# A last layer norm split 704 to 320 columns, with weight and bias in two joined pairs of PSUM banks

## The chip, the cores and the metric

The kernel runs on one core of a Trainium2 chip. The metric is the device time of one launch in microseconds; lower is better. A core has five engines that run their own instruction streams and wait for each other: TensorE (PE, matrix products; its weight loads are shown as PEld), VectorE (DVE), ScalarE (ACT), GpSimd (POOL) and SyncE (SP, which issues most transfers here). [...]

## The reference

One decoder layer on x of 2048 rows x 1024 columns: two mixers, then a mixture of 32 experts, each half closed by a layer norm. The change touches the experts and the second norm:

```python
def hierarchical_moe(h, ...):        # two of the 32 experts for each row
    ...
    def expert_block(args):          # 128 rows of one expert
        xb, e = args
        hid = jax.nn.silu(xb @ w_gate[e]) * (xb @ w_up[e])      # 1024 -> 256
        return hid @ w_down[e]                                  # 256 -> 1024
    ...
# in reference():
        ffn = hierarchical_moe(h, ...)
        x = layer_norm(DEEP_ALPHA * x + gate2 * ffn, ln2_g[l], ln2_b[l])

def layer_norm(x, g, b):             # per row of 1024
    mu = x.mean(-1); var = square(x - mu).mean(-1)
    return (x - mu) * rsqrt(var + LN_EPS) * g + b
```

## The kernel before

The mixers fill the first 1205 us or so. Then `moe()` runs the 32 experts, and `tail()` the last norm.

**Experts.** A block is up to 128 rows of one expert. Every expert e has a block 0; 15 of the 32 have rows enough for a second one, block 1. Whether they do is known only at run time, so all work of a second block stands in arms that are run or skipped (`when`, L1209; the branches are at L1211). A float32 product is done as three products of a high and a low half: a high half is a rounded copy made by ACT, a low half is the difference, made by DVE or POOL.

For a block, PE turns the 128 x 1024 rows into eight 128 x 128 transposes (`turn`, L1116) in two PSUM tiles pT0 and pT1 of four each. `turned` (L1120) then copies each half on ACT (xT_hi, L1125) and subtracts on DVE (xT_lo, L1126). `gate_up` (L1135) is 24 matmuls of 512 columns into pg0 for block 0 or pg1 for block 1. `hidden` is ACT's silu (L1142) and DVE's product (L1143, hid). `hidden_turn` (L1152) turns that into ph, `hidden_turned` splits it (L1158 on ACT, L1159 on DVE), `down` (L1168) is 12 matmuls into two of three tiles pd, and `put` (L1176) has DVE scale them into y in two halves, which POOL adds to memory (`scatter`, L1182). Beside that the weights of the next expert are split: four pieces gu_hi on ACT (L1092) and gu_lo on DVE (L1093), and two pieces dn on ACT (L1101) and POOL (L1102).

The order of the experts' work on each engine is that of the code (`manual_schedule`, L1668). For one expert e PE does gate_up of (e, 0), turn of (e+1, 0), the hidden_turn of (e-1, 1) if there is one, down of (e-1, 0), then, each if there is one, gate_up of (e, 1), down of (e-1, 1) and turn of (e+1, 1), then hidden_turn of (e, 0), and begins gate_up of (e+1, 0). DVE does hT_lo of (e-1, 0), three gu_lo, hid of (e, 0), the two xT_lo of (e+1, 0), the fourth gu_lo, the two y of (e-1, 0), then, each if there is one, hid of (e, 1), y of (e-1, 1) and xT_lo of (e+1, 1).

**Waits.** A tile framework derives the waits between engines from the tiles that instructions read and write. An instruction that depends on work of another engine waits until that engine's count has reached the place of that work. A skipped arm adds the same counts, in its engine's order.

**Last norm.** `tail()` has the 16 row tiles of 128 in SBUF in six groups (TAIL: 1, 2, 3, 4, 3, 3 tiles). For each group the mean and variance come from DVE or ACT, DVE works out the scale in short operations that end at L1525, in scratch columns in PSUM. Then each row tile of 1024 columns is shared: columns up to `TS` go to DVE in two operations (L1537: minus the mean and times g, then times the scale and plus b; g and b lie in pT0 and pT1, copied there by ACT at L1466), the rest are normalised by ACT (L1530) and multiplied by g and added to b by POOL in two operations (L1538). Then the tile is stored (L1540). Here only SP's order is fixed by hand; the other engines' order is set by the framework's scheduler.

Of the kernel before, what the change touches and what calls it, by code (L numbers as in the profile page):

```python
# [10 lines left out]
F32 = mybir.dt.float32  # L11
# [9 lines left out]
P = 128  # L21
D = 1024
SEQ = 2048
KD = D // P
# [11 lines left out]
NG = 4  # L36
NONE = 1 << 20
ADA = 0.4
TS, TAIL = 512, ((1, 1), (2, 1), (3, 1), (4, 1), (3, 1), (3, 1))
HS = 608  # L40

RA, RB, MH2, MH3, WO = 0.6, 1.0, 0.25, 0.5, 0.5
# [11 lines left out]
class Layer:  # L54
# [1135 lines left out]
    def moe(self):  # L1190
# [20 lines left out]
            with tc.If((masks[engines][e // 16] & (1 << e % 16)) > 0):  # L1211
                work()
        PE, AV, DVE, POOL = (E.PE,), (E.Activation, E.DVE), (E.DVE,), (E.Pool,)
        self.pgs = pgs = [self.pk.tile([P, 512], F32, name=f"pg{i}") for i in range(2)]
        self.phs = self.ph.tile([P, 2, P], F32, tag="ph", name="ph")
        self.pds = pds = [self.pk.tile([P, 512], F32, name=f"pd{i}") for i in range(3)]
        self.pTs = [self.pk.tile([P, 4, P], F32, name=f"pT{i}") for i in range(2)]
        self.gate2 = mc.tile([P, D], F32, name="gate2")
        second = [mc.tile([P, D], F32, name=f"hr1_{i}") for i in range(2)]
        hr = [self.hrp.tile([P, D], F32, tag="hr", name="hr") for _ in range(2)]  # L1220
# [3 lines left out]
        for j in range(2):  # L1224
            t = mc.tile([P, NE, 4], I32, name=f"idx{j}")
# [11 lines left out]
        rows, xT, hid, hT, y = {}, {}, {}, {}, {}  # L1237
# [218 lines left out]
    def tail(self):  # L1456

        nc = self.nc
        g, b = self.g2b2
# [1 line left out]
        junk, stats = (self.hrp.tile([P, D], F32, tag="hr", name=n) for n in ("junk", "stats"))  # L1461
        xs, groups = [], []

        rows = [t.rearrange("p a b -> p (a b)") for t in self.pTs]
        for t, r in zip(rows, (g, b)):
            act.activation(t, r[:, 0:TS], AF.Copy)  # L1466
        for i in range(NT // 4):
            x = self.t16([P, 4, D], name="tail_x")
            for j in range(4):
                t = 4 * i + j  # L1470
                nc.sync.dma_start(x[:, j], self.d_xa[t * P:(t + 1) * P])  # L1471
                xs.append(x[:, j])

        t, cols = 0, self.pgs[0]
        for n, nv in TAIL:
            f = stats[:, 64 * len(groups):64 * len(groups) + 64]
            c = cols[:, 16 * len(groups):16 * len(groups) + 16]
# [212 lines left out]
```

## Time and profile before

| | |
|---|---|
| median of 3 runs | 1768.59 us (1767.44 to 1770.77) |
| the profiled execution | 1770.56 us |
| its span | 1768.9 us, mean granted clock of PE 0.956 |
| busy, whole span | PE 1565.4 us (88%), DVE 1254.1 (71%), ACT 775.4 (44%), POOL 534.7 (30%) |
| experts, 1205 to 1672 us | PE 442.84 us of 467 |
| last norm, 1694 us to the end | PE 0 us |

The profile is that of one execution, with start and length of every instruction on each engine. A span runs from the first to the last of them; the execution's own time is a little longer. An idle time in brackets is the engine's wait just before a row, with what released it. PEclk is the clock that TensorE was granted, as a share of full speed.

### The profile page before, as it was taken

What the parts mean: (1) busy time and instruction counts of PE and PEld (TensorE: products, weight loads), DVE (VectorE), ACT (ScalarE), POOL (GpSimd) and SP (SyncE); (2) the same over time, 40 slices, a digit from 0 to 9 for tenths busy, and PEclk for the clock granted to TensorE, in tenths of its full rate; (3) what the DMA queues carried; (4) which work ended last, traced back from release to release, by engine and by line L of the source; (5) the groups of instructions that cost most, each with busy time, mean ns of one, the idle gap of its engine ahead of it and who ended that gap; (6) DMA issues with size and microseconds to landing.
All of it is one profiled execution on the core that took longest, in us unless ns stands there. A gap on an engine that the chain in (4) does not pass through costs nothing. (4 is left out here: it accounts for less than half of the span.)

```text
span 1768.9 us, 25248 instructions
## 1 busy us (share of the span) xinstructions
PE 1565.4 (88%) x7784; PEld 1261.1 (71%) x7784; DVE 1254.1 (71%) x3010; ACT 775.4 (44%) x1603; POOL 534.7 (30%) x441
## 2 busy tenths in 40 slices
PE   6899999998999999999889999957999989999800
PEld 4678877776777778888678888845777778778600
DVE  6777667766877987574688887665667686876554
ACT  4433455445233336344443322226545565554452
POOL 3200111021110003022320211215556675765517
PEclk9999999999999999999999999978999999999955
DMA  9553586455764758544477854347989998998464
GB/s 282 166 184 100 167 249 192 127 136 161 219 198 144 214 163 252 141 99 118 143 241 227 256 168 144 138 160 224 298 259 290 285 316 265 294 305 240 105 221 178
DMA packets 347943, 356.79 MB, mean 202 GB/s; under 512 B 49705, under 2 KB 283778, under 8 KB 347794
## 3 DMA queue, kind: packets, MB, share of 16 engines
q1 hardware_dynamic: 330546, 316.61, 56.4%
q0 software_dynamic: 17248, 38.37, 9.2%
q8 instruction: 71, 1.16, 0.3%
q14 instruction: 78, 0.64, 0.1%
HBM read 268.83 MB, written 101.79 MB: 210 GB/s over the span
## 5 line engine op out<-in xcount | busy, mean ns | idle before, releaser
L280 PE MATMUL acc<-hhi,w_hi 128*128 128x512 f32 x896 | 365.6, 409 | 7.4 <-ACT st L444 3.2
L280 PE MATMUL acc<-hlo,w_hi 128*128 128x512 f32 x896 | 360.6, 403 | 1.7 <-DVE hlo L337 1.0
L280 PE MATMUL acc<-hhi,w_lo 128*128 128x512 f32 x896 | 361.0, 403 | 0.0
L280 PEld LDWEIGHTS acc<-hhi,w_hi 128*128 128x128 f32 x896 | 171.3, 191 | 48.6 <-ACT st L444 4.1
L280 PEld LDWEIGHTS acc<-hlo,w_hi 128*128 128x128 f32 x896 | 170.7, 191 | 40.8 <-DVE hlo L337 2.4
L280 PEld LDWEIGHTS acc<-hhi,w_lo 128*128 128x128 f32 x896 | 170.9, 191 | 39.7 <-issue 1.7
L1093 DVE TENSOR_TENSOR gu_lo<-gu_raw,gu_hi 128x1024 fp32r<-128x1024 f32 (+1 forms) x132 | 179.7, 1404 | 24.1 <-ACT gu_hi L1092 15.7
L1102 POOL TENSOR_TENSOR dn<-dn_raw,dn 128x1024 fp32r<-128x1024 f32 x64 | 168.2, 2655 | 58.4 <-ACT dn L1101 56.1
L1135 PE MATMUL pg<-gu_hi,xT_hi 128*128 128x512 f32 x376 | 150.0, 399 | 1.2 <-ACT xT_hi L1125 1.2
L1135 PE MATMUL pg<-gu_hi,xT_lo 128*128 128x512 f32 x376 | 147.5, 392 | 0.1
L1135 PE MATMUL pg<-gu_lo,xT_hi 128*128 128x512 f32 x376 | 147.3, 392 | 0.0
L1092 ACT ACTIVATE gu_hi<-gu_raw 128x1024 fp32r<-128x1024 f32 (+1 forms) x132 | 129.0, 1035 | 4.6 <-PE mix L889 2.8
L1168 PE MATMUL pd<-dn,hT_hi 128*128 128x512 f32 x376 | 120.6, 402 | 6.2 <-PEq L1211 2.5
L453 DVE SCALAR_TENSOR_TENSOR cv<-st,cw,cv 128x512 f32<-128x512 f32 x144 | 108.5, 754 | 2.1
L1182 POOL DMA_INDIRECT d_xa<-y,idx x47 | 77.1, 1640 | 105.9 <-DVE y L1176 46.3
L889 PE MATMUL mix<-wo_hi,y_hi 128*128 128x512 f32 x256 | 105.1, 411 | 0.0
L889 PE MATMUL mix<-wo_hi,y_lo 128*128 128x512 f32 x256 | 103.6, 404 | 1.2 <-DVE y_lo L871 1.2
L889 PE MATMUL mix<-wo_lo,y_hi 128*128 128x512 f32 x256 | 103.5, 404 | 0.0
L347 ACT ACTIVATE w_hi<-raw 128x1024 fp32r<-128x1024 f32 x56 | 59.6, 1065 | 93.4 <-PE acc L280 75.5
L1126 DVE TENSOR_TENSOR xT_lo<-pT,xT_hi 128x512 fp32r<-128x512 f32 x94 | 60.6, 686 | 39.1 <-ACT xT_hi L1125 35.2
L575 POOL TENSOR_SCALAR_AFFINE_SELECT gam<-gam 128x512 f32<-128x512 f32 x16 | 11.2, 701 | 252.7 <-ACT gam L574 241.7
L1168 PEld LDWEIGHTS pd<-dn,hT_hi 128*128 128x128 f32 x376 | 67.1, 188 | 27.4 <-issue 7.0
(352 smaller groups left out, 3255.1 us busy)
## 6 DMA issues: line engine op xcount, KB each, us to landing
dn_raw<-in_w_down_dram SPq DMA_DIRECT2D x32, 1024.0 KB
gu_raw<-in_w_gate_dram SPq DMA_DIRECT2D x60, 512.0 KB
gu_raw<-in_w_up_dram SPq DMA_DIRECT2D x60, 512.0 KB
raw<-in_w_in_dram SPq DMA_DIRECT2D x56, 512.0 KB
ada_w<-in_w_ada_dram SPq DMA_DIRECT2D x96, 256.0 KB
qkvT<-cv SPq DMA_DIRECT2D x48, 256.0 KB
x_t<-in_x_dram SPq DMA_DIRECT2D x16, 512.0 KB
y_raw<-yT SPq DMA_DIRECT2D x16, 512.0 KB
```

The source lines that it names most:

```text
L280: self.nc.tensor.matmul(ps, a[:, k, :], b[q][:, k, :], start=k + n == 0, stop=k == KD - 1 and n == 2)
L347: nc.scalar.activation(hi, raw, AF.Copy)
L453: nc.vector.scalar_tensor_tensor(y, st[:, t:t + 512], self.cw4[:, j, t:t + 1], y, op0=OP.mult, op1=OP.add)
L575: nc.gpsimd.affine_select(gam, gam, pattern=[[0, H], [1, P]], compare_op=OP.is_ge, fill=0.0, base=0, channel_multiplier=-1)
L889: nc.tensor.matmul(ps, a[:, k, :], self.wo[n][b][:, k, :], start=i == 0, stop=i == 3 * KD - 1)
L1092: nc.scalar.activation(hi[:, c], r, AF.Copy)
L1093: i = nc.vector.tensor_tensor(lo[:, c], r, hi[:, c].bitcast(F32), op=OP.subtract)
L1102: nc.gpsimd.tensor_tensor(dn[:, 1, k], r[:, k], dn[:, 0, k].bitcast(F32), op=OP.subtract)
L1126: nc.vector.tensor_tensor(lo[:, c], pT[n], hi[:, c].bitcast(F32), op=OP.subtract)
L1135: self.nc.tensor.matmul(ps, a[:, k], b[:, k], start=n == 0, stop=n == 3 * KD - 1)
L1168: self.nc.tensor.matmul(ps[n], hT[a][:, k], dn[:, b, k, c], start=i == 0, stop=i == 5)
L1182: i = self.nc.gpsimd.indirect_dma_start(out=self.d_xa, out_offset=bass.IndirectOffsetOnAxis(ap=idx[:, 0:1], axis=0), in_=y, in_offset=None ...
```

## The change

`TS` goes from 512 to 704, so DVE takes 704 columns of a row in the last norm, ACT and POOL 320. [...] So the two tiles pT0 and pT1 become one tile `pT` of two banks, and pg0 and pg1 one tile `pg` of two banks, both used through half views by the experts as before. In the last norm g lies in the first 704 columns of pT and b in those of pg, and the scratch columns move from pg0 to pd0.

```diff
-TS, TAIL = 512, ((1, 1), (2, 1), (3, 1), (4, 1), (3, 1), (3, 1))
+TS, TAIL = 704, ((1, 1), (2, 1), (3, 1), (4, 1), (3, 1), (3, 1))
...
-        self.pgs = pgs = [self.pk.tile([P, 512], F32, name=f"pg{i}") for i in range(2)]
+
+        self.pg = self.pk.tile([P, D], F32, name="pg")
+        self.pgs = pgs = [self.pg[:, i * 512:i * 512 + 512] for i in range(2)]
         self.phs = self.ph.tile([P, 2, P], F32, tag="ph", name="ph")
         self.pds = pds = [self.pk.tile([P, 512], F32, name=f"pd{i}") for i in range(3)]
-        self.pTs = [self.pk.tile([P, 4, P], F32, name=f"pT{i}") for i in range(2)]
+        self.pT = self.pk.tile([P, KD, P], F32, name="pT")
+        self.pTs = [self.pT[:, 4 * i:4 * i + 4] for i in range(2)]
...
-        rows = [t.rearrange("p a b -> p (a b)") for t in self.pTs]
+        rows = [t[:, 0:TS] for t in (self.pT.rearrange("p a b -> p (a b)"), self.pg)]
         for t, r in zip(rows, (g, b)):
             act.activation(t, r[:, 0:TS], AF.Copy)
...
-        t, cols = 0, self.pgs[0]
+        t, cols = 0, self.pds[0]
```

No instruction is added or taken out, and lines behind the experts' tiles count three higher. What moves are waits. On PE, before, between the turn of a second block of the next expert (an arm that may be skipped) and the next expert's first gate_up matmul (the last two rows; hr_1 are the rows of the second block):

```order
L1116 MATMUL pT_11285<-ident,hr_1_11289 128x128 [waits DMASW6_49,DMASW3_49,DMASW7_49,DMASW2_49,DVE_49]
L1116 MATMUL pT_11285<-ident,hr_1_11289 128x128 x3
L1116 MATMUL pT_11286<-ident,hr_1_11289 128x128 [waits DVE_49]
L1116 MATMUL pT_11286<-ident,hr_1_11289 128x128 x3
L1211 UNCONDITIONAL_BRANCH
L1211 UNCONDITIONAL_BRANCH [waits PE_49]
L1152 MATMUL ph<-ident,hid 128x128 [waits DVE_49]
L1152 MATMUL ph<-ident,hid 128x128
L1135 MATMUL pg_11279<-gu_hi,xT_hi 128x512 [waits Activation_49]
L1135 MATMUL pg_11279<-gu_lo,xT_hi 128x512
```

The same place on PE now:

```order
L1116 MATMUL pT<-ident,hr_1_11287 128x128 [waits DMASW6_49,DMASW3_49,DMASW7_49,DMASW2_49,DVE_49]
L1116 MATMUL pT<-ident,hr_1_11287 128x128 x7
L1211 UNCONDITIONAL_BRANCH
L1211 UNCONDITIONAL_BRANCH [waits PE_49]
L1152 MATMUL ph<-ident,hid 128x128 [waits DVE_49]
L1152 MATMUL ph<-ident,hid 128x128
L1211 UNCONDITIONAL_BRANCH
L1135 MATMUL pg<-gu_hi,xT_hi 128x512 [waits DVE_49,Activation_49]
```

The gate_up into pg waited for ACT alone; now it waits for DVE too, up to the place where DVE reads pg for the hid of a second block, which stands behind y of the expert before.

On ACT, the split of a turned second block and what follows, before:

```order
L1211 COMPARE_AND_BRANCH
L1125 ACTIVATE xT_hi<-pT_11285 128x512 [waits DVE_49,PE_49,Activation_49]
L1125 ACTIVATE xT_hi<-pT_11286 128x512 [waits DVE_49,PE_49]
L1211 UNCONDITIONAL_BRANCH
L1211 UNCONDITIONAL_BRANCH [waits Activation_49]
```

The same place on ACT now:

```order
L1211 COMPARE_AND_BRANCH
L1125 ACTIVATE xT_hi<-pT 128x512 [waits DVE_49,PE_49,Activation_49]
L1125 ACTIVATE xT_hi<-pT 128x512 [waits DVE_49]
L1211 UNCONDITIONAL_BRANCH
L1211 UNCONDITIONAL_BRANCH [waits Activation_49]
```

The second copy waited for PE's transposes; now it waits for DVE, up to the xT_lo that reads the first half of the same tile. The same holds where the turned block is a block 0.

In the last norm the last rows of DVE before, around the scale of the last group (L1525):

```order
L1522 SCALAR_TENSOR_TENSOR stats<-pg_11279,stats 128x3 [waits DVE_49]
L1524 COPY pg_11279<-stats 128x3 [waits DVE_49]
L1537 SCALAR_TENSOR_TENSOR tail_x<-tail_x,stats,pT_11286 128x512
L1525 TENSOR_TENSOR stats<-pg_11279,stats 128x3 [waits DVE_49]
L1537 SCALAR_TENSOR_TENSOR tail_x<-tail_x,stats,pT_11286 128x512 x2
```

And now, three lines further down in the file:

```order
L1525 SCALAR_TENSOR_TENSOR stats<-pd_11281,stats 128x3 [waits DVE_49]
L1527 COPY pd_11281<-stats 128x3 [waits DVE_49]
L1540 SCALAR_TENSOR_TENSOR tail_x<-tail_x,stats,pg 128x704
L1528 TENSOR_TENSOR stats<-pd_11281,stats 128x3 [waits DVE_49]
L1540 SCALAR_TENSOR_TENSOR tail_x<-tail_x,stats,pg 128x704 x2
```

Two of DVE's 32 operations stand behind that scale in both.

## Rows read from the trace of the kernel before

**Rows 1.** Windows: stretch, us; busy of PE, PEld, DVE, ACT, POOL; clock; DMA.
```profile
1205.00:1672.00 467.00, 442.84 (x2115) 356.78 (x2116) 322.28 (x393) 256.08 (x369) 291.36 (x153) 1.00 0.88 270
1730.00:1745.00 15.00, 0.00 (x0) 0.00 (x0) 14.00 (x55) 7.32 (x11) 14.66 (x12) 0.50 0.37 147
```
**Rows 2.** Timeline from 1729.5 us: start, us, engine, line, operation, count.
```profile
1730.18 32.41 POOL L1538 TENSOR_TENSOR tail_x<-tail_x,ln 128x512 f32<-128x512 f32 x26 [3.35 <-ACT tail_x L1530]
...
1744.16 0.15 DVE L1525 TENSOR_TENSOR stats<-pg,stats 128x3 f32<-128x3 f32 x1
...
1744.35 2.23 ACT L1530 ACTIVATE tail_x<-tail_x,stats 128x512 f32<-128x512 f32 x3 [2.15 <-DVE stats L1525]
```
**Rows 3.** Lines of the last norm: operation, count; busy us, mean ns; idle before.
```profile
L1538 POOL TENSOR_TENSOR tail_x<-tail_x,ln 128x512 f32<-128x512 f32 x32 | 39.6, 1264 | 36.7 <-ACT tail_x L1530 36.0
L1537 DVE SCALAR_TENSOR_TENSOR tail_x<-tail_x,stats,pT 128x512 f32<-128x512 f32 x32 | 23.2, 735 | 0.2
L1530 ACT ACTIVATE tail_x<-tail_x,stats 128x512 f32<-128x512 f32 x16 | 11.9, 802 | 7.7 <-DVE stats L1525 7.7
```
**Rows 4.** Lines of the experts, 1205 to 1672 us.
```profile
L1102 POOL TENSOR_TENSOR dn<-dn_raw,dn 128x1024 fp32r<-128x1024 f32 x64 | 168.2, 2655 | 58.4 <-ACT dn L1101 56.1 <-DMA d_xa<-y,idx 2.0
L1126 DVE TENSOR_TENSOR xT_lo<-pT,xT_hi 128x512 fp32r<-128x512 f32 x94 | 60.6, 686 | 39.1 <-ACT xT_hi L1125 35.2 <-DVEq L1211 3.2 <-ACT gu_hi L1092 0.7
L1159 DVE TENSOR_TENSOR hT_lo<-ph,hT_hi 128x256 fp32r<-128x256 f32 x45 | 18.8, 419 | 8.5 <-ACT hT_hi L1158 4.3 <-DVEq L1211 3.3 <-ACT gu_hi L1092 0.9
```
**Rows 5.** Timeline of expert 14, 1411.4 to 1419.5 us.
```profile
1411.38 1.22 DVE L1093 TENSOR_TENSOR gu_lo<-gu_raw,gu_hi 128x1024 fp32r<-128x1024 f32 x1
1412.00 5.22 POOL L1102 TENSOR_TENSOR dn<-dn_raw,dn 128x1024 fp32r<-128x1024 f32 x2 [0.21 <-ACT dn L1101]
...
1414.39 1.08 ACT L1125 ACTIVATE xT_hi<-pT 128x512 fp32r<-128x512 f32 x2
...
1415.02 1.29 DVE L1126 TENSOR_TENSOR xT_lo<-pT,xT_hi 128x512 fp32r<-128x512 f32 x2 [0.95 <-ACT xT_hi L1125]
...
1415.59 1.06 ACT L1092 ACTIVATE gu_hi<-gu_raw 128x1024 fp32r<-128x1024 f32 x1
...
1416.69 1.61 DVE L1093 TENSOR_TENSOR gu_lo<-gu_raw,gu_hi 128x1024 fp32r<-128x1024 f32 x1 [0.38 <-ACTq L1211]
...
1418.23 1.27 DVE L1176 TENSOR_TENSOR y<-pd,gate 128x512 f32<-128x512 f32 x2
...
1418.49 0.48 PE L1135 MATMUL pg<-gu_hi,xT_hi 128*128 128x512 f32 x1
```
**Rows 6.** Timeline of expert 15, 1427.5 to 1433 us.
```profile
1427.77 3.24 DVE L1093 TENSOR_TENSOR gu_lo<-gu_raw,gu_hi 128x1024 fp32r<-128x1024 f32 x1 [0.38 <-ACTq L1211]
...
1429.66 0.48 PE L1135 MATMUL pg<-gu_hi,xT_hi 128*128 128x512 f32 x1
...
1430.93 1.27 DVE L1176 TENSOR_TENSOR y<-pd,gate 128x512 f32<-128x512 f32 x2
```
**Rows 7.** Timeline of expert 8, 1329.5 to 1337 us.
```profile
1335.16 1.27 DVE L1176 TENSOR_TENSOR y<-pd,gate 128x512 f32<-128x512 f32 x2
...
1336.37 0.48 PE L1135 MATMUL pg<-gu_hi,xT_hi 128*128 128x512 f32 x1
```
**Rows 8.** Timeline of expert 0, 1212 to 1216.5 us.
```profile
1214.52 1.29 DVE L1126 TENSOR_TENSOR xT_lo<-pT,xT_hi 128x512 fp32r<-128x512 f32 x2 [0.88 <-ACT xT_hi L1125]
...
1214.55 0.50 PE L1135 MATMUL pg<-gu_hi,xT_hi 128*128 128x512 f32 x1
```
**Rows 9.** Timeline of expert 13, 1399 to 1407.5 us.
```profile
1404.71 1.27 DVE L1176 TENSOR_TENSOR y<-pd,gate 128x512 f32<-128x512 f32 x2
...
1405.44 0.73 PE L1168 MATMUL pd<-dn,hT_hi 128*128 128x512 f32 x2
```
**Rows 10.** Timeline between experts 9 and 10, 1350.5 to 1353 us.
```profile
1352.03 0.48 DVE L1143 SCALAR_TENSOR_TENSOR hid<-pg,idx,hid 128x256 f32<-128x256 f32 x1 [2.98 <-ACT hid L1142]
...
1352.40 0.48 PE L1135 MATMUL pg<-gu_hi,xT_hi 128*128 128x512 f32 x1
```

## Prediction

> **What bounds the kernel now.** I read the windows view first, cut at the stages. In the 467 us of the experts the matmuls of PE are busy for 442.84 us, at a granted clock of 1.00, DVE for 322 and POOL for 291 [rows 1]: the experts are bound by PE, and every new wait of PE there is paid, unless PE would have waited anyway. In the last norm PE is idle. From 1730 to 1745 us POOL is busy for 14.66 of 15 us and DVE for 14.00 [rows 1]. The timeline then shows what ends last: POOL's 26 last additions and multiplications run without a gap for 32.41 us to 1762.59, while DVE has finished its last scale at 1744.31 [rows 2]. The span is 1768.9, so the last store and the end take 6.3 us after POOL. The last norm is bound by POOL, whose queue is still long when DVE is done.
>
> The profiled execution took 1770.56 us; the median is 1768.59, 1.97 lower. The sum below is a difference against the profiled execution and is then set on the median.
>
> **The last norm.** A half-row operation on POOL takes 1264 ns at 512 columns, on DVE 735, on ACT 802 [rows 3]. POOL goes from 512 to 320 columns. Its wider row, 1024 columns in 2655 ns [rows 4], shows no fixed share (2.59 ns a column against 2.47), so 320 columns are 0.79 us by proportion; I take 0.83. DVE gets 192 columns more. Two of its subtractions out of PSUM, 512 columns in 686 ns and 256 in 419 ns [rows 4], give 1.04 ns a column, so +0.20 us each, 0.94 in all. ACT's normalisation of 320 columns becomes some 0.63.
>
> 30 of DVE's 32 operations stand ahead of the last group's scale, as in the two order pieces of the tail: that scale moves from 1744.31 by 30 x 0.20 = 6.0 to 1750.3. ACT's first tile is ready at 1750.95. POOL has just caught up by then: it starts its run some 4 us later than 1730.18 (20 of the 30 operations lie ahead), and 20 operations of 0.83 end at 1750.8. Its last six, for three tiles, end at 1750.95 + 6 x 0.83 = 1755.9; with a hand-off at the start, 1756.1. Against 1762.59 that is **-6.5**. DVE becomes the last norm's bound.
>
> Bounds: if POOL's price did not shrink with the width, the tail would end as before plus POOL's later start, +4. If DVE's growth were hidden, the last scale stays at 1744.31 and POOL's six end at 1749.9, -12.7. No row shows DVE reading 704 columns across two banks. If the second bank costs a second start (419 ns less 256 x 1.04 is 0.15 us), the 30 operations give 4.5 back and -2 is left; nothing speaks for it, I take no cost. The two copies into PSUM are 192 columns longer and run before the rows arrive: nothing.
>
> **The joined tiles in the experts.** A tile is what the order of dependent work is kept by. Two half tiles were followed apart; a joined one is followed as one. The order pieces show two new waits.
>
> First, ACT's second half copy xT_hi now waits for DVE's xT_lo of the first half. At expert 14 the two copies took 1.08 us together from 1414.39, DVE's two 1.29 from 1415.02 [rows 5]. So the second copy can start only at 1415.02 + 0.69 [rows 4] = 1415.71 with a wake, and ends at 1416.35, 0.88 later than 1415.47. What stands behind it on ACT is the fourth gu_hi, and behind that on DVE the fourth gu_lo and then y.
>
> Second, PE's gate_up of the next expert waits for DVE up to the hid of a second block, which stands behind y of the previous expert; where there is no second block, the skipped arm releases it, and only once DVE has done y. Before, PE needed ACT's xT_hi alone and DVE could be late. Behind the waiting matmul stands all of PE's work.
>
> What a late y costs is read at expert 14: y ends at 1419.50, PE started the gate_up of 15 at 1418.49 [rows 5], so 1.01 of waiting, plus what the first wait adds. The fourth gu_lo would start at 1416.69 + 0.88 = 1417.57. It took 1.61 us, while one beside which POOL began late took 1.22, and it ended 1.08 after POOL's dn, which ran to 1417.22 [rows 5]. Started after that, it takes 1.22 and ends at 1418.79, 0.49 later than before; I use 0.47 everywhere.
> [...]
>
> With 0.1 for the release, the terms are:
> - Experts 14, 15 and 21, no turn of a second block between: 1.01 + 0.47 + 0.1 = 1.55 each, **4.65**. At 15 the plain reading is larger: y ended at 1432.20 and PE began at 1429.66 [rows 6], 2.54 late, behind a gu_lo of 3.24 us. But PE's waiting at 14 lets DVE catch up, so only the increase counts.
> - Experts 1, 8, 11, 16 and 22, where a turn of a second block takes PE's time: at 8, the one of the five that is shown, y ended at 1336.43 and PE began at 1336.37 [rows 7], 0.06 + 0.57 = 0.63. By the same pair of rows 11 gives 0.71 and 1 gives 0.91; 16 and 22, once what went before is paid, 0.6 each: **3.45**. At 30, y is early: nothing.
> - Expert 0, with no y: the xT_lo pair ends at 1215.81, PE began at 1214.55 [rows 8]; 1.26 + 0.88 + 0.1 = **2.2**.
> - Seven experts after one with a second block (4, 7, 10, 13, 20, 24, 29): the gate_up comes late enough, but the second half of the second block's down waits for the first half of y; at 13 y began at 1404.71 and the matmuls at 1405.44 [rows 9], right behind it. y is 0.47 later: **3.3**.
> - Three gate_ups right behind a hid of the second block, as at 1352.51 against 1352.40 [rows 10], 0.2 each: **0.6**.
>
> The sum is **+14.2**. Lower bound: the first wait is swallowed, and what is left is 1.01 three times, the small lateness of the others and 2.2 + 0.6, about 6.5. Upper bound: the lateness at 15 and at three more of that pattern, 16, 21 and 22 (2.54, 3.2, 2.65, 1.8 by the same pair of rows) stands in full with 0.88 each, 13.7, beside the 1.55 of 14, 2.2 for three others and the last three terms, 6.1: 23.6, about 24. PE has such short waits already with its clock at 1.00 over the stage [rows 1]; I charge no clock. Loads and POOL's gathers move along with PE.
>
> **Sum**: +14.2 - 6.5 = +7.7, 1778.3 for the profiled execution. On the median: **1776.3**.
>
> **Rivals.**
> 1. The lateness of DVE stands in full. For it: gu_lo of 3.24 us [rows 6] shows that POOL's dn can hold DVE, and after a shift it may hold it elsewhere. Against: PE's waits give DVE time. 1768.6 + 24 - 6.5 = 1786.
> 2. The waits are small, and the norm pays for them: the lower bound, 6.5 - 6.5, 1768.6, no change. For it: PE's shift moves the whole ring, and a place that is late once is early next.
> 3. The other side: the joined tiles bring no order. The two halves lie in different banks, and if the engines run beside each other in them, as xT_hi's second half and xT_lo's first do now from 1415.02 to 1415.47 [rows 5], only the norm counts: 1768.59 - 6.5 = 1762.1. It decides if PE's first matmul of an expert starts before y ends. Against it stand the waits in the order pieces.
> [...]
> 4. The norm's gain fails, by DVE's second start or POOL's price: 1768.6 + 14.2 - 2 to + 4, 1781 to 1787.
>
> **Chances.** The forecast 0.60; rival 1 0.14; rival 2 0.13; rival 3 0.08; rival 4 0.05. The forecast's own range is 1772 to 1782 (experts +10 to +20, norm -6.5). The range is 1765 to 1786: it goes down past rival 2 with a norm of -9 (1768.6 + 6.5 - 9 = 1766), and up to rival 1; rival 3 lies below, and little above. What can't be told from no change is 0.2%, 3.5 us. Slower: the forecast, rivals 1 and 4, 0.77 with a little lost to the forecast's lower edge, 0.76. Same: rival 2's, 0.13. Faster: 0.11, rival 3 and the low part of rival 2.
>
> **What would show it.** Right: PE waits ahead of the first gate_up matmul after experts 0, 1, 8, 11, 14, 15, 16, 21 and 22, released by DVE, 0.6 to 2.2 us each; ACT's two xT_hi apart by an xT_lo; the last down matmul some 14 us later; POOL's operation in the norm near 0.83 us, DVE's near 0.94, the norm 6.5 us shorter, with POOL done soon after DVE's last scale. Wrong: PE starts those matmuls while y runs; the experts' stage is as long as before; or POOL's operation stays above 1.1 us.

## The result

The changed kernel takes 1789.59 us (median of four, 1784.70 to 1795.56) against 1768.69 for the kernel before: a ratio of 1.0118, interval 1.0079 to 1.0158. It is slower, as forecast, but by about 21 us where 7.7 were forecast, and above the range of 1765 to 1786.

The profiled execution took 1795.56 us, 25.00 more than that of before. Cut at the first gate_up matmul of expert 0 and the last matmul of expert 31, the difference falls into three parts: expert 0's gate_up begins 6.42 us later (1211.70 against 1205.28), the experts take 502.42 us against 478.51 (1205.28 to 1683.79 in the kernel before; [rows 1] stops at 1672), +23.91, and what follows is 5.33 shorter. 6.42 + 23.91 - 5.33 = 25.00. The first part is not the change: the instructions of each engine ahead of the experts are the same in both, and in the runs below that start lies anywhere from 1198.5 to 1211.8, in kernels with and without the change. Why it moves these runs don't tell. It is a good part of the scatter between executions: a second profile of the changed kernel has that start 10.0 us earlier and took 1786.58 us, 9.0 less. So the experts are compared here by their own stretch.

The windows of the changed kernel, the whole of its experts first, then pieces around the wait at expert 14 (stretch, us; busy of PE, PEld, DVE, ACT, POOL; granted clock; DMA):

```profile
1211.70:1714.10 502.40, 462.81 (x2154) 369.23 (x2154) 319.35 (x401) 261.25 (x372) 290.94 (x155) 0.98 0.83 252
1432.90:1436.08 3.18, 0.55 (x4) 0.24 (x3) 2.49 (x4) 1.87 (x4) 0.21 (x1) 1.00 0.57 181
1436.08:1437.30 1.22, 1.22 (x5) 1.01 (x6) 0.50 (x2) 1.22 (x2) 1.15 (x1) 1.00 1.11 384
1437.30:1440.70 3.40, 3.40 (x9) 2.63 (x8) 3.33 (x3) 1.59 (x2) 2.79 (x3) 0.50 1.03 342
1440.70:1442.00 1.30, 1.30 (x7) 1.08 (x6) 0.00 (x0) 0.00 (x0) 1.28 (x2) 0.99 0.89 178
```

The clock over the experts was 1.00 in [rows 1]; it is 0.98 now. PE was busy for 0.55 of the 3.18 us up to the gate_up of expert 15. It began that at 1.00, and 1.2 us later, in the midst of dense work, fell to 0.50 for 3.40 us. The 24 matmuls of that gate_up took 7.31 us from first to last, against 5.72 before: 1.6 us lost behind the wait, about as much as the wait.

The timeline of expert 14 in the changed kernel, for [rows 5]:

```profile
1430.29 0.59 ACT L1125 ACTIVATE xT_hi<-pT 128x512 fp32r<-128x512 f32 x1
...
1430.91 0.69 DVE L1126 TENSOR_TENSOR xT_lo<-pT,xT_hi 128x512 fp32r<-128x512 f32 x1 [0.95 <-ACT xT_hi L1125]
...
1431.64 0.60 ACT L1125 ACTIVATE xT_hi<-pT 128x512 fp32r<-128x512 f32 x1 [0.76 <-DVE xT_lo L1126]
...
1432.27 0.69 DVE L1126 TENSOR_TENSOR xT_lo<-pT,xT_hi 128x512 fp32r<-128x512 f32 x1 [0.66 <-ACTq L1211]
1432.36 1.06 ACT L1092 ACTIVATE gu_hi<-gu_raw 128x1024 fp32r<-128x1024 f32 x1
1433.45 1.23 DVE L1093 TENSOR_TENSOR gu_lo<-gu_raw,gu_hi 128x1024 fp32r<-128x1024 f32 x1 [0.49 <-ACTq L1211]
...
1434.22 0.41 PE L1152 MATMUL ph<-ident,hid 128*128 128x128 f32 x2 [1.19 <-PEq L1211]
1434.59 1.28 DVE L1176 TENSOR_TENSOR y<-pd,gate 128x512 f32<-128x512 f32 x2
...
1436.08 0.47 PE L1135 MATMUL pg<-gu_hi,xT_hi 128*128 128x512 f32 x1 [1.44 <-ACT gu_hi L1092]
```

Both new waits are there: the two copies of xT_hi stand apart with an xT_lo between them, and PE begins 0.21 us after y has ended (1434.59 + 1.28 = 1435.87). Before, PE began 1.01 us ahead of that end. The releaser named in the last bracket, ACT's gu_hi, is only what came last in the profile; gate_up doesn't read that piece; what it follows is y, by 0.20 to 0.21 us at all eight gate_ups that come to wait for one. The gu_lo, which begins 0.34 us after POOL's dn has ended (1433.11), takes 1.23 us where it took 1.61.

For [rows 7], [rows 9] and [rows 8], the timelines of experts 8, 13 and 0:

```profile
1348.43 1.28 DVE L1176 TENSOR_TENSOR y<-pd,gate 128x512 f32<-128x512 f32 x2
1349.92 0.47 PE L1135 MATMUL pg<-gu_hi,xT_hi 128*128 128x512 f32 x1 [0.48 <-ACT xT_hi L1125]
...
1420.59 1.28 DVE L1176 TENSOR_TENSOR y<-pd,gate 128x512 f32<-128x512 f32 x2
1421.33 0.73 PE L1168 MATMUL pd<-dn,hT_hi 128*128 128x512 f32 x2 [0.43 <-DVE y L1176]
...
1222.42 0.69 DVE L1126 TENSOR_TENSOR xT_lo<-pT,xT_hi 128x512 fp32r<-128x512 f32 x1 [0.66 <-ACTq L1211]
...
1223.31 0.76 PE L1135 MATMUL pg<-gu_hi,xT_hi 128*128 128x512 f32 x1 [2.19 <-ACT hT_hi L1158]
...
1223.87 0.63 PE L1135 MATMUL pg<-gu_lo,xT_hi 128*128 128x512 f32 x1
```

At each PE begins just behind DVE. Matmuls of 0.63 us, as in the last row, are those at the clock of 0.50; at 1.00 they show 0.39, as in the same kernel's gate_up of 15 from 1440.95 on.

The last norm: its groups of instructions by line (busy us, mean ns), then the last scale and POOL's last 20 operations, for [rows 3] and [rows 2]:

```profile
L1541 POOL TENSOR_TENSOR tail_x<-tail_x,ln 128x320 f32<-128x320 f32 x32 | 27.1, 861 | 43.6 <-DVE pd L1506 28.3 <-ACT tail_x L1533 14.1
L1540 DVE SCALAR_TENSOR_TENSOR tail_x<-tail_x,stats,pT 128x704 f32<-128x704 f32 x16 | 14.9, 932 | 1.0 <-ACT junk L1496 0.7 <-issue 0.2
L1533 ACT ACTIVATE tail_x<-tail_x,stats 128x320 f32<-128x320 f32 x16 | 9.4, 644 | 15.0 <-DVE stats L1528 14.8
```

```profile
1769.97 17.62 POOL L1541 TENSOR_TENSOR tail_x<-tail_x,ln 128x320 f32<-128x320 f32 x20 [0.28 <-ACT tail_x L1533]
...
1780.67 0.16 DVE L1528 TENSOR_TENSOR stats<-pd,stats 128x3 f32<-128x3 f32 x1
```

DVE's wide operation takes 932 ns, as 735 and 192 columns of 1.04 ns make 935, so no price for the second bank is to be seen; POOL's 861, ACT's 644. The last scale ends 66.7 us after the experts' last matmul, POOL 73.5 us after it, against 78.8 before.

### The profile page after: what moved, and what is told of

The parts are those of the page before. It is cut to its first block, busy times and chain, and to the rows that moved or that the text cites. A ratio compares the mean times of both kernels' runs of the same rounds, so it can differ in the third digit from the quotient of the medians.

```text
span 1793.8 us, 25232 instructions
## 1 busy us (share of the span) xinstructions
PE 1581.3 (88%) x7784; PEld 1271.5 (71%) x7784; DVE 1252.0 (70%) x3010; ACT 777.2 (43%) x1603; POOL 516.6 (29%) x441
## 5 line engine op out<-in xcount | busy, mean ns | idle before, releaser
L1093 DVE TENSOR_TENSOR gu_lo<-gu_raw,gu_hi 128x1024 fp32r<-128x1024 f32 (+1 forms) x132 | 167.0, 1308 | 30.1 <-ACT gu_hi L1092 24.0
L1126 DVE TENSOR_TENSOR xT_lo<-pT,xT_hi 128x512 fp32r<-128x512 f32 x94 | 65.0, 692 | 75.6 <-ACT xT_hi L1125 58.9
L1135 PEld LDWEIGHTS pg<-gu_hi,xT_hi 128*128 128x128 f32 x376 | 73.0, 194 | 28.9 <-ACT gu_hi L1092 4.5
L1125 ACT ACTIVATE xT_hi<-pT 128x512 fp32r<-128x512 f32 x94 | 56.2, 598 | 80.4 <-DVE xT_lo L1126 39.8
```

The costliest lines, as they stand in the source:

```text
L1093: i = nc.vector.tensor_tensor(lo[:, c], r, hi[:, c].bitcast(F32), op=OP.subtract)
L1125: self.last_turn = nc.scalar.activation(hi[:, c], pT[n], AF.Copy)
L1126: nc.vector.tensor_tensor(lo[:, c], pT[n], hi[:, c].bitcast(F32), op=OP.subtract)
L1135: self.nc.tensor.matmul(ps, a[:, k], b[:, k], start=n == 0, stop=n == 3 * KD - 1)
```

## The experiments

The theory was that the experts lose some 24 us: 16 to 17 of waits of PE, and 7.2 because the clock falls behind the four longest of them. A rival was that the joined tiles slow the mixers, a second that the clock falls for another reason, a third that part of the loss is the norm's. Times of the experts below are from expert 0's first gate_up matmul to the last matmul, in the profile: 478.51 us before.

**The change again.**

> The changed kernel once more. Theory: the experts cost some 24 us more (about 16.5 us of new waits of PE on DVE and ACT, and 7.2 us because the granted clock falls to 0.50 for some 3 us behind the four longest waits), the last norm gives 5.3 back, and the 6.4 us by which the first transposes of the experts began later in the profiled run (1209.08 against 1202.66) are not the change but differ from run to run: median 1784 to 1796, and in this profile the first transpose stands anywhere from 1202 to 1210. Rival: the joined tiles also slow the mixers ahead of the experts; then the first transpose is at 1208 or later again.

Measured: 1789.13 us, ratio 1.0095 (1.0070 to 1.0121). Expert 0's gate_up began at 1201.70, 3.6 us earlier than in the kernel before (the first transpose, at 1199.08, even ahead of the stretch expected), and still the experts took 503.64 us, +25.1. The rival of slower mixers is out. The clock fell behind the same four gate_ups, which took 7.4 us more together, in other shares: 2.9 at 16 and 1.3 at 1.

**The joins alone.**

```diff
-TS, TAIL = 704, ((1, 1), ...
+TS, TAIL = 512, ((1, 1), ...
```

> Both joins, but TS stays 512, so the last norm is shared as before. Theory: the whole loss of the experts stands and the norm gives nothing back: the changed kernel plus 5.3, some 1768.7 + 24 = 1792 (1789 to 1799). Rival: part of the loss belongs to the wider rows of the norm; then it lies below the changed kernel.

Measured: 1795.88 us, ratio 1.0133 (1.0093 to 1.0172); experts 504.62 us, +26.1; POOL ended 80.0 us after the last matmul. The loss is there in full without the wide rows, so it is the joins', and the wide rows are worth 6.5 us (80.0 against 73.5).

**The wide rows without the joins.** The experts' PSUM pools are closed after `moe()`, and the norm opens one of its own:

```diff
+            with ExitStack() as ps:
+                self.ph = self.pool(ps, name="ph", bufs=1, space=PSUM)
+                self.pk = self.pool(ps, name="pk", bufs=1, space=PSUM)
...
+            self.pn = self.pool(st, name="pn", bufs=1, space=PSUM)
...
+        rows = [self.pn.tile([P, D], F32, name=n)[:, 0:TS] for n in ("g2", "b2")]
...
+        t, cols = 0, self.pn.tile([P, 512], F32, name="cols")
```

> TS is 704, but the experts keep their separate half tiles; the norm gets two PSUM tiles of two banks of its own once the experts' pools are closed. Theory: the experts are as before and the norm is 5.3 us shorter: 1768.7 - 5.3 = 1763.4 (1761 to 1766). Rival: the norm's gain needs the early copy of weight and bias into tiles that the experts free one by one, or the wide rows cost something else: 1768 or more.

Measured: 1767.49 us against 1773.19 for the kernel before, measured beside it, ratio 0.9974 (0.9953 to 0.9996). The experts took 479.11 us, as before, and POOL ended 72.1 us after them, 6.7 earlier. So the change's purpose can be had without its price.

**y ahead of the fourth gu_lo**, in the changed kernel:

```diff
-                for _ in su:
-                    pass
                 if e:
                     down(e - 1, 0)
                     out(e - 1, 0)
                     store(e - 1, 0)
+                for _ in su:
+                    pass
```

> The changed kernel, but y of the expert before stands ahead of the fourth gu_hi and gu_lo on ACT and DVE. Theory: PE's waits ahead of gate_up of experts 15, 16 and 22 (1.7, 1.6 and 2.8 us) fall below 0.7, the clock stays at 1.00 behind them (4.8 us), five waits of 0.7 and seven of 0.5 on y go too: some 15 us below the changed kernel, 1775 (1772 to 1780). Rival: the clock falls for a reason other than the length of PE's wait, or the fourth gu_lo is now late for the 18th matmul: 1782 or more.

Measured: 1778.32 us, ratio to before 1.0028 (1.0013 to 1.0043), 10.8 below the changed kernel measured beside it; one of its twelve executions took 7083.71 us, which I can't explain. So it came within the range expected, but not by the way expected. The seven downs behind y, 0.5 us longer in the changed kernel, are 0.1 to 0.2 shorter than in the kernel before. But PE still waited 1.42, 1.35 and 1.64 us ahead of gate_up of 15, 16 and 22, where less than 0.7 was expected, and still 2.24 ahead of that of 1, where there is no y. Its timeline at expert 14 shows why:

```profile
1423.02 1.29 DVE L1176 TENSOR_TENSOR y<-pd,gate 128x512 f32<-128x512 f32 x2 [0.23 <-PEq L1211]
...
1424.22 1.21 DVE L1093 TENSOR_TENSOR gu_lo<-gu_raw,gu_hi 128x1024 fp32r<-128x1024 f32 x1
...
1425.64 0.49 PE L1135 MATMUL pg<-gu_hi,xT_hi 128*128 128x512 f32 x1 [1.18 <-DVEq L1211]
```

PE now waits for the gu_lo, and begins 0.21 us behind its end: what it waits for is the skipped arm of the second block's hid, which stands behind whatever DVE does last. The windows around the two gate_ups of 15 and 22, from the end of the matmuls before:

```profile
1422.86:1425.64 2.78, 0.41 (x4) 0.23 (x3) 2.42 (x3) 1.47 (x3) 1.13 (x2) 1.00 0.79 245
1425.64:1426.00 0.36, 0.36 (x2) 0.32 (x3) 0.00 (x0) 0.36 (x2) 0.36 (x1) 0.93 1.09 373
1426.00:1429.30 3.30, 3.30 (x9) 2.57 (x8) 2.93 (x4) 2.72 (x3) 2.69 (x3) 0.50 1.08 384
```

```profile
1530.40:1533.40 3.00, 0.41 (x4) 0.24 (x3) 2.64 (x3) 1.69 (x3) 2.83 (x2) 1.00 0.86 256
1533.40:1539.00 5.60, 5.60 (x25) 4.57 (x26) 4.88 (x4) 2.98 (x4) 5.27 (x3) 1.00 1.01 341
```

Behind the first the clock fell to 0.50 within 0.4 us, and it fell at 1 and 16 too; behind the second, in which PE was idle for a little longer, it stayed at 1.00. How long PE waits does not settle by itself whether the clock falls.

**One join at a time**, on the kernel before.

```diff
-        self.pTs = [self.pk.tile([P, 4, P], F32, name=f"pT{i}") for i in range(2)]
+        self.pT = self.pk.tile([P, KD, P], F32, name="pT")
+        self.pTs = [self.pT[:, 4 * i:4 * i + 4] for i in range(2)]
```

> The kernel before with pT0 and pT1 joined and nothing else: ACT's second xT_hi half waits for DVE's first xT_lo half, PE's gate_up for ACT alone. Theory: only the seven places where the second half of a second block's down waits for y pay (0.5 each), and expert 1 at its start: 3 to 6 us in the experts, no wait over 1 us ahead of a gate_up after expert 1, and the clock stays. Rival: the serial halves on ACT and DVE are the main loss, 12 or more.

Measured: 1770.72 us, ratio 0.9997 (0.9977 to 1.0018). The experts took 485.28 us, +6.8 and a little above the forecast: 0.5 to 0.9 at the seven downs, 1.05 and 0.71 at two turns (behind the gate_ups of 17 and 22) that the forecast did not have, no wait of over 1 us ahead of a gate_up, no lower clock behind one. That it cost nothing in all is the norm: POOL ended 71.3 us after the experts, 7.5 earlier than before, at the same width. The scheduler, which orders all but SP there, had put ACT's first normalised tile further ahead, before sums of later groups; it began at 1708.58 where it was 1712.54, with the experts' last matmul at the same time in both:

```profile
1708.58 0.81 ACT L1531 ACTIVATE tail_x<-tail_x,stats 128x512 f32<-128x512 f32 x1
...
1722.60 32.52 POOL L1539 TENSOR_TENSOR tail_x<-tail_x,ln 128x512 f32<-128x512 f32 x26 [2.54 <-ACT tail_x L1531]
```

POOL's 26 last operations are as long as in [rows 2], but begin at 1722.60 where it was 1730.18.

```diff
-        self.pgs = pgs = [self.pk.tile([P, 512], F32, name=f"pg{i}") for i in range(2)]
+        self.pg = self.pk.tile([P, D], F32, name="pg")
+        self.pgs = pgs = [self.pg[:, i * 512:i * 512 + 512] for i in range(2)]
```

> The kernel before with pg0 and pg1 joined and nothing else: PE's gate_up waits for y, but y itself isn't made later. Theory: at experts 1, 15, 16 and 22 PE waits some 1.3, 1.1, 1.1 and 2.2 us, at the others 0.2 to 0.4, 7 to 9 in all, and the clock falls behind fewer than four of them: 8 to 14 us in the experts. Rival: the two waits bite only together, since PE waits where y is late by both; then it is below 4.

Measured: 1784.59 us, ratio 1.0073 (1.0046 to 1.0101); experts 492.55 us, +14.0, the upper end. PE waited 1.47, 1.22, 0.92 and 2.84 us at 1, 15, 16 and 22, and behind all four, not fewer, the gate_up took 1.2 to 2.5 us more, 6.9 together. So here waits of about 1 us cost as much again in clock. The two joins alone add up to 20.8 us; together they cost 23.9, 25.1 and 26.1 in the three profiles.

**PE kept busy while it waits**, in the changed kernel:

```diff
-                self.hidden_turn(hid[e, 0])
+                for _ in range(7 if e in (0, 14, 15, 21) else 1):
+                    self.hidden_turn(hid[e, 0])
```

> The changed kernel, but at experts 0, 14, 15 and 21 PE does hidden_turn seven times in place of once (the same values into ph), so it has work while gate_up of the next expert waits. The output is the same. Theory: the clock falls because PE is idle; gate_up of 15, 16 and 22 starts as late as in the changed kernel (within 0.5 us), but its 24 matmuls run at a granted clock of 1.00, 1.6 us less each: 4 to 8 us below the changed kernel. Rival: the clock falls behind a late start for another reason; then each of these gate_ups again takes 1.6 us more, and the kernel is no faster, or slower by the later hT_hi.

Measured: 1785.45 us, ratio to before 1.0063 (1.0032 to 1.0094); experts 495.25 us, 7.2 less than in the changed kernel's profile. Expert 14, timeline and then windows:

```profile
1429.11 1.72 PE L1152 MATMUL ph<-ident,hid 128*128 128x128 f32 x14 [1.30 <-PEq L1211]
1429.36 1.28 DVE L1176 TENSOR_TENSOR y<-pd,gate 128x512 f32<-128x512 f32 x2
...
1430.85 0.47 PE L1135 MATMUL pg<-gu_hi,xT_hi 128*128 128x512 f32 x1
```

```profile
1427.50:1430.85 3.35, 2.03 (x17) 1.54 (x15) 2.66 (x4) 0.69 (x1) 0.38 (x1) 1.00 0.57 189
1430.85:1436.40 5.55, 5.55 (x24) 4.54 (x25) 3.92 (x4) 4.17 (x5) 4.86 (x3) 1.00 1.07 314
```

Gate_up still begins 0.21 us after y, as late as without the extra work (1.7 us of shift at expert 14, now 1.31 of transposes and 0.4 of waiting), but it runs at 1.00 throughout. So did those of 1, 16 and 22. That shows the clock's part: with PE at work in the four waits it stayed at 1.00, and the experts took 7.2 us less. The times agree less sharply: ratios of 1.0063 and 1.0095 to the kernel before are some 6 us apart, and their intervals overlap.

**A version that beats both.** Separate tiles, the wide norm in tiles of its own, and y ahead of the fourth gu_lo:

> Separate half tiles in the experts, the wide norm in PSUM tiles of its own, and y ahead of the fourth gu_hi and gu_lo. Theory: as the separate-tile kernel with TS of 704, and the seven waits of down on y fall by 0.2 to 0.4 us each: 1.5 to 3 below it, some 6 to 9 below the kernel before. Rival: those waits are hidden or the fourth gu_lo comes late: the same as the separate-tile kernel or worse.

Measured: 1766.14 us against 1772.59, ratio 0.9961 (0.9945 to 0.9978). The experts took 476.91 us, 2.2 less than in the separate-tile kernel: 1.6 of it are the seven downs, 0.2 each.

The last three test the norm's order, with ACT's order there written out by hand:

```diff
-            with self.tc.manual_schedule(engines={mybir.EngineType.SP}):
+            with self.tc.manual_schedule(engines={E.SP, E.Activation}):
```

> The kernel before with TS 512 and one thing changed: in the last norm ACT keeps the order of the code, so its normalised columns of the first groups stand ahead of the sums of later groups. With pT alone joined the scheduler came upon nearly this order, and POOL's 26 last operations then began 45.6 us after the experts' last matmul instead of 46.4 plus 7 of later start (1722.60 against 1730.18 at the same end of the experts). Theory: POOL's stream, which bounds this norm at TS 512, begins earlier and the norm ends 6 to 8 us sooner: a ratio near 0.996. Rival: what shortened the norm was the joined weight tile or chance; then no change.

(The 45.6 us in it are a slip; by the two rows named there, it is 1722.60 - 1683.80 = 38.8 against 46.4.) Measured: ratio 0.9980 (0.9967 to 0.9994), half of what was expected; in the profile POOL ended 78.0 us after the experts, 0.8 earlier, since ACT, bound to the code's order, now waited 7.77 us for the first scale, and what stood behind it waited too.

> Separate half tiles in the experts, y ahead of the fourth gu_lo, the norm's own PSUM tiles, ACT's norm in the order of the code, TS 608. Theory: POOL starts early and has 416 columns, DVE's 0.10 us a row operation costs 3 us: the norm ends 65 to 68 us after the experts, 11 to 13 below the kernel before in all, with the 1.5 of the experts 12 to 15 below. Rival: DVE bounds the norm as soon as POOL starts early, and the order gives nothing more than at 704: 6 to 8 below.

Measured: 1765.23 us, ratio 0.9966 (0.9951 to 0.9981); POOL ended 76.0 us after the experts, not 65 to 68. The theory missed.

> The same with TS 704. Theory: at 704 the norm is bound by DVE, so ACT's order gives little: 72 us after the experts, as without it, 7 to 9 below the kernel before. Rival: POOL's late start also held this one, then it is as fast as TS 608 or faster.

Measured: 1763.63 us, ratio 0.9959 (0.9943 to 0.9975); POOL ended 73.9 us after the experts. It is level with the same kernel without ACT's order. That order by hand is no gain, and why the scheduler's order with pT joined was better by 7.5 us is open: I did not get it without the join.

## Why the prediction was wrong

**The step that failed** is the sentence "PE has such short waits already with its clock at 1.00 over the stage [rows 1]; I charge no clock". The clock fell to 0.50 at four of PE's new waits, ahead of the gate_ups of 1, 15, 16 and 22, for 6.8 us at the first and 3.4 at each of the others, and these gate_ups took 2.39, 1.59, 1.59 and 1.61 us longer, 7.18 in all. At 1 it fell while PE still waited:

```profile
1222.26:1223.31 1.05, 0.00 (x0) 0.03 (x1) 0.69 (x1) 0.63 (x3) 0.90 (x2) 0.50 0.74 156
1223.31:1229.09 5.78, 5.78 (x14) 4.52 (x15) 3.92 (x4) 3.66 (x4) 4.68 (x3) 0.50 1.07 366
```

The run with PE kept busy gets these 7.2 us back with the waits still in place. I had read that PE's existing gaps of 1.2 us left the clock alone (in the kernel before it is below 1.00 only in the first 3.5 us of the experts), and not that the new wait comes on top of such a gap: behind the down of expert 13 the kernel before already leaves PE nothing but two transposes, 1.19 us after that down; the new wait stands right behind them, so that in the 3.18 us up to the gate_up PE worked for 1.99 before and for 0.55 now. From the kernel before, a row of its timeline and the window:

```profile
1418.33 0.41 PE L1152 MATMUL ph<-ident,hid 128*128 128x128 f32 x2 [1.19 <-DVE gu_lo L1093]
```

```profile
1415.31:1418.49 3.18, 1.99 (x11) 1.35 (x10) 2.80 (x4) 1.23 (x2) 1.91 (x1) 1.00 0.91 306
```

The four falls came at stretches with little work: in the 3.18 us up to the gate_ups of 1, 15, 16 and 22 PE was busy for 0.41, 0.55, 0.54 and 0.41. With 2.03 of 3.35 us up to the gate_up of 15, in the run with PE kept busy, the clock stayed at 1.00.

**The waits** were mis-sized little, 14.2 forecast and 16.1 in the changed kernel's profile: the 16.4 of the table, of which 0.3 came back. Measured is how much later each place begins, counted from the matmul ahead of it, than in the kernel before; that is up to 0.25 us more than the idle time in the rows, since PE's matmuls overlapped there before (by 0.25 ahead of the gate_up of 15: 1418.33 + 0.41 against 1418.49).

| place | forecast | measured |
|---|---|---|
| gate_up of 1 | 2.2 | 2.24 |
| gate_up of 15, 16, 22 | 1.55 each, 4.65 | 1.69, 1.63, 2.84; 6.16 |
| gate_up of 2, 9, 12, 17, 23 | 3.45 | 0.64, 0.73, 0.84, 0.84, 0.76; 3.81 |
| seven downs behind y | 3.3 | 0.41 to 0.56; 3.5 |
| three behind a hid | 0.6 | 0.21, 0.25, 0.25; 0.7 |

At 22 the lateness of 2.65 stood in full, as rival 1 had it, and 0.3 of it came back at the next turn; at 16, 17 and 23 the rule that only the increase counts was nearly right. At 15 the 1.69 is the old 1.01, the 0.47 by which y comes later, as the fourth gu_lo begins 0.87 us later against the hidden_turn but takes 1.23 where it took 1.61, and 0.21 from y to PE, where 0.1 was taken for the release. (1.01 + 0.47 + 0.1 is 1.58, not the 1.55 of the prediction.) Both traces show gu_lo shorter behind POOL's dn than beside it, where it stands alone in a row: in the kernel before, 29 of 30 end 1.07 to 1.10 us after dn and take 1.54 to 4.70 us (the 3.24 of [rows 6] is one, with dn ending at 1429.92); in the changed kernel those beside dn take 2.08 to 2.38 us, those that begin 0.34 us or more after it 1.22 or 1.23.

**The norm** was forecast at -6.5: it is 5.3 shorter against the kernel before, 6.5 against the joins alone and 6.7 with separate tiles. DVE's 0.94 and ACT's 0.63 were right, and DVE's last scale came 66.7 us after the last matmul where 66.5 was forecast. But POOL had not caught up by then, and DVE did not become the bound: POOL ran its last 20 operations without a gap from 1769.97, with four tiles still to do at that scale. They took 0.88 us from one to the next where 0.83 was taken, and over 26 operations that makes the 1.2 that is missing.

**The sum by these terms**: 16.1 + 7.2 and 0.6 of small shifts make the 23.9 of the experts; less 5.3 is +18.6, where +7.7 was forecast. The rest of the 25 us of the profiled run is the 6.4 ahead of the experts, which is no property of the change: in its second profile the changed kernel began them earlier than the kernel before. Measured again, the medians are 15.9 us apart, and the forecast with 7.2 for the clock would have been +14.9. The range's upper end was +17.4, so that the first median lies above it is in part the scatter of that start; that the experts lose 23.9 to 26.1 us in three profiles, where 14.2 were forecast, is not.

**The rivals.** Rival 1's time, 1786, is nearest, but the lateness it named gives 1.3 us of the miss; the clock gives 7.2. So that time is near by luck. Rival 2's small waits and rival 4's lost norm did not come: 16.1 and -5.3. Rival 3, no waits at all, is refuted by every gate_up that begins behind y: in the kernel before the engines work side by side in the two halves, for 0.45 us at expert 14 [rows 5], but the program with joined tiles has them wait.

## What to carry to other kernels

A tile is also what the waits are kept by: two buffers that are joined for a later stage, for their size, are ordered as one in every stage that uses their halves. Give the later stage a pool of its own, or check on the engine that sets the pace what its first instruction behind the join now waits for, skipped branches included. Where PE sets the pace and gets a new wait next to a gap that it has already, don't take the clock for free: here the four longest waits, 8.4 us, cost 7.2 more in clock, and those of 0.85 us and less nothing. Look for work to put into the gap, or read the clock in a trace.

## What the runs showed that I had not expected

- In the five profiles with pg joined and no extra work for PE, the clock fell to 0.50 at 19 of the 20 longest waits, of 0.92 to 2.84 us, and the gate_up behind took 1.2 to 2.9 us more. The fall set in between 1.4 us before PE began again and 1.2 us after. The one exception is a stretch with PE busy for 0.41 of 3.00 us, while one with 0.41 of 2.78 was followed by it; and in the run of the joins alone the clock fell once more, at the gate_up of 31, without such a wait. What decides these runs don't tell.
- The same mixers, instruction for instruction, let the experts begin between 1198.5 and 1211.8 us from the span's start.
- With a join in a tile that the norm reads, the scheduler put ACT's work in the last norm in another order and the norm ended 7.5 us sooner, more than the 192 columns gave that the change is about. That the order did it is not shown: written out by hand it gave 0.8.
